# Square roots of the layer norms on ScalarE, and a retention product in three products of parts: one change to a decoder layer on one Trainium2 core

## The chip, the cores and the metric

The kernel runs on one core of a Trainium2 chip. The core has a matrix engine (TensorE, in the profile PE, its weight loads PEld), two engines for elementwise work that matter here (VectorE, DVE, and ScalarE, ACT), a GpSimd engine (POOL) that is all but unused, and a SyncE (SP) that issues most of the DMAs. Each engine works off its own list of instructions in order and waits on semaphores for the others. The metric is the time of one execution in microseconds (us), as the median of several runs.

## The reference, cut to what matters

The layer takes 256 tokens of width 2048. All arrays are float32.

```python
h = layer_norm(alpha * h + 0.5 * swiglu(h, w_ffn1_gu, w_ffn1_down), ln_g[0], ln_b[0])
rq, rk, rv, rg, aq, ak, av, gate_r, gate_a = split(h @ w_in)
ro = head_group_norm(retention_chunkwise(rotary(rq), rotary(rk) * RET_DK**-0.5, rv), ret_gn_g)
ret_branch = (silu(rg) * ro) @ w_ret_out
att_branch = sliding_window_attention_sinks(rotary(aq), rotary(ak), av, att_sinks) @ w_att_out
mixed = (sigmoid(gate_r) * ret_branch + sigmoid(gate_a) * att_branch) @ w_mix_out
h = layer_norm(alpha * h + mixed, ln_g[1], ln_b[1])
h = layer_norm(alpha * h + 0.5 * swiglu(h, w_ffn2_gu, w_ffn2_down), ln_g[2], ln_b[2])
ple = sigmoid(h @ w_ple_gate) * (p @ w_ple_proj)
h = layer_norm(alpha * h + ple, ln_g[3], ln_b[3])
```

`layer_norm` is `(x - mean) * rsqrt(var + 1e-5) * g + b` over the 2048 columns of a token. The retention has 8 heads with keys of 128 and values of 256 columns: a head's output for token t is the sum over s <= t of `gamma**(t-s) * (q_t . k_s) * v_s`, and each head's output is normalized over its 256 columns.

## The kernel before, in words

**Products in parts.** A float32 number is taken as a high part (rounded to the type float32r, which TensorE takes in one pass) and a low part, the remainder, also float32r. `split` (L97) makes both: ScalarE copies the value into the high part, VectorE subtracts it from the value. A product of two such pairs is the sum of three products, low by high, high by high and high by low, in `Sum.add` (L374 to L376). Nearly all of TensorE's work is of this kind, with a weight tile that streams from memory, is split on arrival and is used once. A planner (`plan`, `fill`, `take`, `done`) loads and splits weight chunks ahead of their use, within a budget of buffers; a chunk of weights is 128 by 1024 numbers, its split one ACT and one DVE instruction. After each chunk (a unit of 12 products) `run_side` takes one job from the list `side`; small work that has no stage of its own goes there.

**The layer norms.** There are four, for two halves of 128 tokens (t = 0 and 1) each. Norms 0, 1 and 2 go through the class `Norm`. `held_out` (L506) runs the last product of the stage before for the tokens of t = 0 first, keeping its weight chunks, then `normal(0)` computes the norm of t = 0 on VectorE while TensorE goes through the kept chunks again for t = 1. A written list of events says after which steps `turn` takes place: TensorE transposes 512 normalized columns into a PSUM bank (L593), and `split` makes the next stage's input of them. `normal(1)` follows at the event "sums". The next stage's first chunks are then used in the same order (`first`): t = 0 while the norm of t = 1 is still being made, then t = 1. With norms 0 and 1 a further small product with the embeddings p (`put_by`) stands between the two stages; its results are copied out of PSUM by ScalarE (L737).

`normal(t)` adds the last block of sums (L613), takes its statistics (`bn_stats`, L614), aggregates mean and variance (L576), and calls `rsqrt` (L531) for `1 / sqrt(var + eps)`: eight dependent VectorE instructions on one number per token, which begin with a guess from the bits of the number (L536, L541, L543) and improve it twice (L548, L557, L559, and L548, L561). Then `ln_normal` (L581) applies center-and-multiply (L585) and scale-and-add (L586) to two pieces of 256 columns. The other columns follow in `more`, in pieces of 512.

**The last norm** (`embedding`). The half t = 0 is normalized and stored while TensorE still works on the last product for t = 1. For t = 1, `last_half` (L1465) lets TensorE apply the scale of three blocks of columns: the sums of the block before come from ScalarE's sigmoid (L1428) and VectorE (L1430 to L1432); `ln_stats` gives mean and `rstd`; a row of minus the mean (L1473) and of the deviation (L1474) is transposed by TensorE (L1479), split (L1481, L1484), multiplied with the rows of g and b (L1486) and scaled by `rstd` (L1493, L1495) on the way out.

**The retention.** The values rv (2 blocks of 128 tokens by 2048 columns) are computed in four blocks of 512 columns, and `values` (L1067) copies each out of PSUM in float32. A head's work is a chain of jobs in `side`: `ret1` multiplies keys by queries in float32 (L1111, L1112; 128 by 256 and 128 by 128 scores) and the result by the decay (L1115, L1116); `ret2`, one unit later, multiplies the scores by the values in float32 (L1125 to L1127, three products of 256 columns) and takes statistics; `ret2b`, one more unit later, calls `rsqrt` for both token blocks and normalizes. Two heads follow each other, so six jobs make two heads. These jobs run beside the gate product rg (groups `w_in_f2`), 8 units for two heads, and beside `av` and the first attention features. `ret2c`, `ret3` and `ret3b` gate, transpose and split the result.

**Function tables.** ScalarE loads a table when it changes between functions of different sets. The profiled execution has five such loads: for Silu at the start, for Exp (attention), Sigmoid (gates), Silu (second feed-forward) and Sigmoid (embedding).

Of the kernel before, what the change touches and what calls it, by code (L numbers as in the profile page):

```python
# [8 lines left out]
F32 = mybir.dt.float32  # L9
# [46 lines left out]
def layer(ctx: ExitStack, tc: tile.TileContext, io):  # L56
# [16 lines left out]
    def slot(shape, dt, name):  # L73
        return slots.tile(shape, dt, tag="slot", name=name)
# [456 lines left out]
    def rsqrt(dst, var, n, eps):  # L531
# [7 lines left out]
        )  # L539
        s = small.tile([P, n], I32, tag=f"ns{n}", name="ns")  # L540
        dve.tensor_scalar(s, v[:, 0].bitcast(I32), 1, None, ALU.logical_shift_right)  # L541
        y = small.tile([P, n], I32, tag=f"ny{n}", name="ny")
        dve.tensor_scalar(y, s, -1.0, float(0x5F3759DF - 2**31), ALU.mult, ALU.add)  # L543
# [36 lines left out]

    def ln_normal(y, t, mv, rstd, g, b, k0, nk):  # L581

        x = y[k0 // 4][:, t, k0 % 4 * P : (k0 % 4 + nk) * P]
        at = slice(k0 % 8 * P, (k0 % 8 + nk) * P)
        dve.scalar_tensor_tensor(x, x, mv[:, 0:1], g[k0 // 8][:, at], ALU.subtract, ALU.mult)  # L585
        dve.scalar_tensor_tensor(x, x, rstd, b[k0 // 8][:, at], ALU.mult, ALU.add)  # L586

    def ln_turn(y, t, i, new, k0, nk, keep=None):
# [12 lines left out]
    class Norm:  # L601
# [75 lines left out]
        def first(self, steps, lhs, sums, events):  # L677
# [70 lines left out]
    sink = const.tile([P, HA], F32, name="sink")  # L748
    trig = {}
    ht = big.tile([P, KD, 512], F32R, tag="ht", name="xt")  # L750

# [302 lines left out]
    def mixers(ht, norm, residual, keepers, away):  # L1054
# [52 lines left out]
        def ret1(h):  # L1107
            def f():
# [7 lines left out]
                dve.tensor_tensor(s[:, S:], ps[:, 1, :P], d[:, S:], ALU.mult)  # L1116
                keep["s", h] = s
            return f

        def ret2(h):  # L1120
            def f():
                s = keep.pop(("s", h))
                v = rv[h // 2][:, :, h % 2 * DV : h % 2 * DV + DV]
                ps = bank(f"ro{h}").rearrange("p (a b) -> p a b", a=2)
                pe.matmul(ps[:, 0, :DV], s[:, :P], v[:, 0], start=True, stop=True)  # L1125
# [51 lines left out]
        both = lambda a, b: lambda: (a(), b())  # L1177
        side.append(ret1(0))
        side.append(ret2(0))
        side.append(ret2b(0))  # L1180
        side.append(ret1(1))
        side.append(ret2(1))
        side.append(ret2b(1))
        for h in range(0, HR, 2):
# [12 lines left out]
            if h + 2 < HR:  # L1197
                for n in (h + 2, h + 3):
                    side.append(ret1(n))
                    side.append(ret2(n))  # L1200
                    side.append(ret2b(n))
        aq = [slot([P, 4, S], F32, f"aq{j}") for j in range(2)]
# [218 lines left out]
    def embedding(ht, norm, y):  # L1421
# [43 lines left out]
        def last_half():  # L1465
# [127 lines left out]
    with tc.manual_schedule():  # L1593
        warm = small.tile([P, 1], F32, tag="nc1", name="warm")
        dve.memset(warm, 0.0)
        act.activation(warm, warm, AF.Silu)
        plan_ffn("f1")
# [113 lines left out]
```

## Time and profile before

| what | value |
|---|---|
| median of 3 runs | 2283.61 us (2283.5 to 2283.78) |
| profiled execution, its own time | 2284.39 us |
| span of its instructions | 2282.6 us |
| DVE busy | 1980.0 us, 87% of the span, 2575 instructions |
| ACT busy | 1204.9 us, 53%, 1455 instructions |
| DMA read and written | 478.67 MB and 25.17 MB, 221 GB/s over the span |
| granted TensorE clock | 0.998 |

The profiled execution took 0.78 us more than the median, and its span is 1.79 us shorter than its own time. The profile says of each instruction when it started, how long it took, and what ended the idle time of its engine before it. Matmuls overlap in the pipeline and their ends are modelled, so the distance between two starts is the safer measure on PE.

### The profile page before, as it was taken

The numbers are of one execution on the slowest core, as the hardware profiler recorded it, in microseconds if no ns is written. First come the engines' busy times: TensorE is split into PE (matmuls) and PEld (weight loads), VectorE is DVE, ScalarE is ACT, GpSimd is POOL, SyncE is SP. The second block draws the span as 40 slices with busy tenths as digits, with TensorE's granted clock in tenths as the row PEclk, the third lists the DMA queues.
The fourth block names the chain that finished last, engine by engine and source line by source line (L and its number), as shares of the span: only waits on it lengthen the run. The fifth ranks groups of instructions, "written<-read, shape, count | busy, mean of one in ns | idle before, by whom it ended". The sixth has DMA issues, their size and how long they took to land.

```text
span 2282.6 us, 29021 instructions
## 1 busy us (share of the span) xinstructions
PE 2266.4 (99%) x10471; PEld 1879.7 (82%) x10471; DVE 1980.0 (87%) x2575; ACT 1204.9 (53%) x1455; POOL 2.2 (0%) x9
## 2 busy tenths in 40 slices
PE   9999999999999999999999999999999999999998
PEld 7888888888888888888778888888888888888876
DVE  7999999999989886778789787789999999889877
ACT  5555555556554443535556454555555555555533
POOL 0000000000000000000000000000000000000000
PEclk9999999999999999999999999999999999999999
DMA  8666665665577788655456567777767766565772
GB/s 299 200 207 197 197 211 179 205 202 192 210 284 274 242 304 307 221 161 163 139 157 233 173 221 271 291 272 237 261 221 253 254 199 216 185 220 194 277 259 74
DMA packets 207592, 505.75 MB, mean 222 GB/s; under 512 B 16076, under 2 KB 19788, under 8 KB 207448
## 3 DMA queue, kind: packets, MB, share of 16 engines
q1 hardware_dynamic: 205320, 501.06, 65.3%
q10 hardware_dynamic: 2128, 2.84, 0.4%
q8 instruction: 82, 1.34, 0.2%
q14 instruction: 62, 0.51, 0.1%
HBM read 478.67 MB, written 25.17 MB: 221 GB/s over the span
## 4 chain that ended last, share of the span: by engine, by line
PE 96%; DVE 2%; DMA 1%; issue 0%; ACT 0%; ACTq 0%; DVEq 0%
PE f1g L376 3%; PE f1g L374 3%; PE f1g L375 3%; PE f2g L376 3%; PE f2g L374 3%; PE f2g L375 3%; PE rqk L325 3%; PE f1u L376 2%; PE f1u L374 2%; PE f1u L375 2%; PE f2u L376 2%; PE f2u L374 2%; PE f2u L375 2%; PE aqk L325 2%; PE f2d L374 2%; PE f1d L374 2%
## 5 line engine op out<-in xcount | busy, mean ns | idle before, releaser
L99 DVE TENSOR_TENSOR lf_gu<-rf_gu,hf_gu 128x1024 fp32r<-128x1024 f32 (+1 forms) x276 | 325.3, 1211 | 14.0 <-ACT hf_gu L98 13.2
L98 ACT CAST hf_gu<-rf_gu 128x1024 fp32r<-128x1024 f32 (+1 forms) x276 | 275.5, 1043 | 31.6 <-DMA rf_gu<-in_f_gu 30.7
L99 DVE TENSOR_TENSOR lf_down<-rf_down,hf_down 128x1024 fp32r<-128x1024 f32 x152 | 181.3, 1220 | 23.4 <-ACT hf_down L98 21.1
L99 DVE TENSOR_TENSOR lw_in_f<-rw_in_f,hw_in_f 128x1024 fp32r<-128x1024 f32 x140 | 167.5, 1218 | 35.7 <-ACT hw_in_f L98 35.7
L98 ACT CAST hf_down<-rf_down 128x1024 fp32r<-128x1024 f32 x152 | 155.4, 1050 | 75.7 <-DMA rf_down<-in_f_down 22.2
L98 ACT CAST huf_gu<-uf_gu 128x1024 fp32r<-128x1024 f32 x70 | 73.8, 1054 | 144.9 <-DVE uf_gu L171 142.0
L98 ACT CAST hw_in_f<-rw_in_f 128x1024 fp32r<-128x1024 f32 x140 | 139.2, 1050 | 4.2 <-DMA rw_in_f<-in_w_in_f 1.8
L374 PE MATMUL f1g<-hf_gu,xt 128*128 128x512 f32 x247 | 96.3, 390 | 0.7 <-ACT hf_gu L98 0.7
L376 PE MATMUL f1g<-lf_gu,xt 128*128 128x512 f32 x247 | 96.4, 390 | 0.0
L375 PE MATMUL f1g<-hf_gu,xt 128*128 128x512 f32 x247 | 96.1, 389 | 0.0
L98 ACT CAST hvf_gu<-vf_gu 128x1024 fp32r<-128x1024 f32 x70 | 73.8, 1055 | 29.8 <-DVE vf_gu L173 28.9
L912 ACT ACTIVATE eve<-eve 128x1024 f32<-128x1024 f32 x20 | 21.2, 1061 | 126.8 <-DVE eve L911 126.8
L374 PE MATMUL f2g<-hf_gu,ht 128*128 128x512 f32 x223 | 86.9, 390 | 0.0
L376 PE MATMUL f2g<-lf_gu,ht 128*128 128x512 f32 x223 | 86.8, 389 | 0.0
L375 PE MATMUL f2g<-hf_gu,ht 128*128 128x512 f32 x223 | 86.8, 389 | 0.0
L99 DVE TENSOR_TENSOR luf_gu<-uf_gu,huf_gu 128x1024 fp32r<-128x1024 f32 x70 | 85.3, 1218 | 0.0
L99 DVE TENSOR_TENSOR lvf_gu<-vf_gu,hvf_gu 128x1024 fp32r<-128x1024 f32 x70 | 85.2, 1218 | 0.0
L374 PE MATMUL f1u<-hf_gu,xt 128*128 128x512 f32 x212 | 83.3, 393 | 0.0
L375 PE MATMUL f1u<-hf_gu,xt 128*128 128x512 f32 x212 | 82.5, 389 | 0.0
L376 PE MATMUL f1u<-lf_gu,xt 128*128 128x512 f32 x212 | 82.5, 389 | 0.0
L374 PE MATMUL f2u<-hf_gu,ht 128*128 128x512 f32 x180 | 71.3, 396 | 0.0
L376 PE MATMUL f2u<-lf_gu,ht 128*128 128x512 f32 x180 | 70.1, 390 | 0.0
(1431 smaller groups left out, 6491.2 us busy)
## 6 DMA issues: line engine op xcount, KB each, us to landing
rf_gu<-in_f_gu SPq DMA_DIRECT2D x358, 512.0 KB
rf_down<-in_f_down SPq DMA_DIRECT2D x176, 512.0 KB
rw_in_f<-in_w_in_f SPq DMA_DIRECT2D x148, 512.0 KB
rw_rv<-in_w_rv SPq DMA_DIRECT2D x32, 512.0 KB
rw_ret<-in_w_ret SPq DMA_DIRECT2D x32, 512.0 KB
rw_mix<-in_w_mix SPq DMA_DIRECT2D x32, 512.0 KB
rw_pg<-in_w_pg SPq DMA_DIRECT2D x32, 512.0 KB
rw_att<-in_w_att SPq DMA_DIRECT2D x16, 512.0 KB
```

The costliest lines, as they stand in the source:

```text
L98: act.copy(dst_hi, src)
L99: (lo_engine or dve).tensor_tensor(dst_lo, src, dst_hi, ALU.subtract)
L325: pe.matmul(ps[f], hi[:, kk, f * P : (f + 1) * P], rhs(k), start=k == 0, stop=k == n_k - 1,)
L374: pe.matmul(o, al, bh, start=first, stop=False)
L375: pe.matmul(o, ah, bh, start=False, stop=False)
L376: pe.matmul(o, ah, bl, start=False, stop=self.left == 0)
L912: act.activation(g, g, AF.Silu)
```

## The change

Both halves of norms 0 to 2, and the half t = 1 of the last, get their root from ScalarE: `root = sqrt(4 * var + 4 * eps)`, then VectorE takes the reciprocal and makes one Newton step, four VectorE instructions in all where there were eight. Between the aggregation and the reciprocal VectorE centers the first 256 columns. `Norm.run` loads the table of Sqrt with a one-element activation at its start, and `Norm.first` loads that of the next function at its end. The half t = 0 of the last norm and the heads' norms keep `rsqrt`.

In the retention, `values` splits the values into parts, a new job `ret1b` splits the scores, and `ret2` makes nine products of parts (three for each of the three blocks) in place of three float32 products. The jobs of two heads are interleaved: five entries of `side` instead of six, with two units between a head's `ret1` and its `ret2`.

The tiles `ns` and `ny` get two buffers instead of three, `warm` moves into a constant tile beside the two biases of the roots.

```diff
+    def ln_stats_by_root(stats, i, t, eps, between):
+        mv = small.tile([P, 2], F32, tag="mv", name=f"mv{i}{t}")
+        dve.bn_aggr(mv, stats.rearrange("p a b -> p (a b)"))
+        root = small.tile([P, 1], F32, tag="nq1", name="nroot")
+        act.activation(root, mv[:, 1:2], AF.Sqrt, bias=roots[eps], scale=4.0)
+        v = small.tile([P, 1], F32, tag="nb1", name="nv")
+        dve.tensor_scalar(v, mv[:, 1:2], eps, -4.0, ALU.add, ALU.mult)
+        between(mv)
+        cur = small.tile([P, 1], F32, tag="nc1", name="ncur")
+        dve.reciprocal(cur, root)
+        b = small.tile([P, 1], F32, tag="nh1", name="nb")
+        dve.tensor_scalar(b, cur, cur, v, ALU.mult, ALU.mult)
+        rstd = small.tile([P, 1], F32, tag="rstd", name=f"rstd{i}{t}")
+        dve.scalar_tensor_tensor(rstd, b, 3.0, cur, ALU.add, ALU.mult)
+        return mv, rstd
+
+    def table_of(f):
+        act.activation(warm, warm, f)
...
         def normal(self, t):
             self.columns(t, len(self.cols) - 1)
-            self.mvr[t] = ln_stats(self.stats[:, t], self.i, t, self.eps)
-            for k0 in (0, 2):
-                ln_normal(self.y, t, *self.mvr[t], *self.vectors, k0, 2)
+            g, b = self.vectors
+            self.mvr[t] = ln_stats_by_root(
+                self.stats[:, t], self.i, t, self.eps, lambda mv: ln_center(self.y, t, mv, g, 0, 2)
+            )
+            ln_scale(self.y, t, self.mvr[t][1], b, 0, 2)
+            ln_normal(self.y, t, *self.mvr[t], g, b, 2, 2)
...
             self.vectors = vectors.pop()
+            table_of(AF.Sqrt)
...
             self.put_away()
+            table_of(AF.Silu if self.i < 2 else AF.Sigmoid)
...
         def values(blk, ps):
-            v = slot([P, 2, 512], F32, f"rvs{blk}")
-            act.copy(v[:, 0], ps[0])
-            dve.tensor_copy(v[:, 1], ps[1])
-            rv.append(v)
+            hi, lo = (slot([P, 2, 512], F32R, f"rv{w}{blk}") for w in "hl")
+            for t in range(2):
+                split(hi[:, t], lo[:, t], ps[t])
+            rv.append((hi, lo))
...
+        def ret1b(h):
+            def f():
+                s, parts = keep.pop(("w", h)), slot([P, 2, 384], F32R, f"rsp{h}")
+                split(parts[:, 0], parts[:, 1], s)
+                keep["s", h] = parts
+            return f
...
-                pe.matmul(ps[:, 0, :DV], s[:, :P], v[:, 0], start=True, stop=True)
-                pe.matmul(ps[:, 1, :DV], s[:, P:S], v[:, 0], start=True, stop=False)
-                pe.matmul(ps[:, 1, :DV], s[:, S:], v[:, 1], start=False, stop=True)
+                for t, blks in ((0, ((0, 0),)), (1, ((P, 0), (S, 1)))):
+                    for col, tk in blks:
+                        at = slice(col, col + P)
+                        for a, b in ((1, 0), (0, 0), (0, 1)):
+                            pe.matmul(
+                                ps[:, t, :DV], s[:, a, at], v[b][:, tk],
+                                start=(a, tk) == (1, 0) and col != S, stop=b == 1 and (t, col) in ((0, 0), (1, S)),
+                            )
...
+        def two_heads(h):
+            side.append(ret1(h))
+            side.append(both(ret1b(h), ret1(h + 1)))
+            side.append(both(ret1b(h + 1), ret2(h)))
+            side.append(both(ret2b(h), ret2(h + 1)))
+            side.append(ret2b(h + 1))
...
-            mv, rstd = ln_stats(stats[:, 1], 3, 1, LN_EPS)
+            mv, rstd = ln_stats_by_root(stats[:, 1], 3, 1, LN_EPS, lambda mv: None)
```

More of the change, by code (lines that the diff above doesn't have):

```diff
@@ L539, in rsqrt @@
         )
-        s = small.tile([P, n], I32, tag=f"ns{n}", name="ns")
+        s = small.tile([P, n], I32, tag=f"ns{n}", name="ns", bufs=2)
         dve.tensor_scalar(s, v[:, 0].bitcast(I32), 1, None, ALU.logical_shift_right)
-        y = small.tile([P, n], I32, tag=f"ny{n}", name="ny")
+        y = small.tile([P, n], I32, tag=f"ny{n}", name="ny", bufs=2)
         dve.tensor_scalar(y, s, -1.0, float(0x5F3759DF - 2**31), ALU.mult, ALU.add)
@@ L579, in ln_stats, with ln_center @@
         return mv, rstd
-    def ln_normal(y, t, mv, rstd, g, b, k0, nk):
+    def ln_stats_by_root(stats, i, t, eps, between):
[15 more added lines that the diff above has]
+        act.activation(warm, warm, f)
+    def ln_center(y, t, mv, g, k0, nk):
         x = y[k0 // 4][:, t, k0 % 4 * P : (k0 % 4 + nk) * P]
@@ L585, in ln_normal, with ln_scale @@
         dve.scalar_tensor_tensor(x, x, mv[:, 0:1], g[k0 // 8][:, at], ALU.subtract, ALU.mult)
+    def ln_scale(y, t, rstd, b, k0, nk):
+        x = y[k0 // 4][:, t, k0 % 4 * P : (k0 % 4 + nk) * P]
+        at = slice(k0 % 8 * P, (k0 % 8 + nk) * P)
         dve.scalar_tensor_tensor(x, x, rstd, b[k0 // 8][:, at], ALU.mult, ALU.add)
+    def ln_normal(y, t, mv, rstd, g, b, k0, nk):
+        ln_center(y, t, mv, g, k0, nk)
+        ln_scale(y, t, rstd, b, k0, nk)
     def ln_turn(y, t, i, new, k0, nk, keep=None):
@@ L749, in layer @@
     trig = {}
+    few = const.tile([P, 3], F32, name="few")
+    warm = few[:, 0:1]
+    roots = {LN_EPS: few[:, 1:2], 4 * LN_EPS: few[:, 2:3]}
     ht = big.tile([P, KD, 512], F32R, tag="ht", name="xt")
@@ L1116, in f @@
                 dve.tensor_tensor(s[:, S:], ps[:, 1, :P], d[:, S:], ALU.mult)
-                keep["s", h] = s
+                keep["w", h] = s
+            return f
[4 more added lines that the diff above has]
+                keep["s", h] = parts
             return f
@@ L1122, in f @@
                 s = keep.pop(("s", h))
[L1123 removed]
+                v = [x[:, :, h % 2 * DV : h % 2 * DV + DV] for x in rv[h // 2]]
                 ps = bank(f"ro{h}").rearrange("p (a b) -> p a b", a=2)
[L1125 to L1127 removed]
+                for t, blks in ((0, ((0, 0),)), (1, ((P, 0), (S, 1)))):
[6 more added lines that the diff above has]
+                            )
                 st = small.tile([P, 2, 6], F32, tag="gst", name=f"gst{h}")
@@ L1197, in mixers @@
             if h + 2 < HR:
[L1198 to L1201, printed above, removed]
+                two_heads(h + 2)
         aq = [slot([P, 4, S], F32, f"aq{j}") for j in range(2)]
@@ L1593, in layer @@
     with tc.manual_schedule():
-        warm = small.tile([P, 1], F32, tag="nc1", name="warm")
         dve.memset(warm, 0.0)
+        for eps, v in roots.items():
+            dve.memset(v, 4.0 * eps)
         act.activation(warm, warm, AF.Silu)
```

7 lines of the change are left out of this document (1 added, 6 removed).

## The prediction

> **What bounds the kernel now.** I read three views in this order: the page's busy times, the table of who waited for whom with TensorE as the waiting engine, and the timeline at those places. The columns of the second are: who waits, for whom, us in total, times, longest.
>
> ```profile
> PE 2266.4 (99%) x10471; PEld 1879.7 (82%) x10471; DVE 1980.0 (87%) x2575; ACT 1204.9 (53%) x1455; POOL 2.2 (0%) x9
> ```
>
> ```profile
> PE plnt L1479 <- DVE plnm L1474: 3.7, 1, 3.7
> PE lnps L593 <- DVE mixy L586: 1.9, 4, 0.7
> ...
> PE pg L374 <- DVE ht L99: 1.1, 1, 1.1
> ...
> PE lnps L593 <- DVE f2y L586: 0.6, 2, 0.3
> ```
>
> The reader is to see that TensorE is busy in 99% of the span. Whatever is gained must therefore be either TensorE's own work, or one of its few waits, or a piece of the tail behind its last big product. The waits all stand at layer norms, for a VectorE chain that ends in L586 or L1474. The change touches all three kinds, and nothing else in it can move the end unless it makes TensorE wait anew.
>
> **The retention's products.** One head, and the 256-column products of `av`, on TensorE's timeline (start, duration, line):
>
> ```profile
> 895.74 0.39 PE L376 MATMUL rg<-lw_in_f,ht 128*128 128x512 f32 x1
> 895.97 0.59 PE L1125 MATMUL ro<-rvs,rsc 128*128 128x256 f32 x2
> ...
> 897.49 0.39 PE L375 MATMUL rg<-hw_in_f,ht 128*128 128x512 f32 x1
> ```
>
> ```profile
> 992.29 0.28 PE L374 MATMUL av<-hw_av,ht 128*128 128x256 f32 x1
> ...
> 995.17 0.60 PE L1111 MATMUL rs<-rq,rk 128*128 128x256 f32 x2
> ```
>
> Two steps of the big product take 2 x 0.23 us (895.74 to 895.97 is one), and here 1.75 us pass from L376 to the second product behind the job; so a head's three float32 products cost 1.29 us, 0.43 each. The second fence holds 24 products of parts of 256 columns, each with its own weights, between 992.29 and 995.17: 0.12 us each. Nine of these are 1.08 us. The change **removes 0.21 us per head, 1.7 us for eight**, on TensorE's own path.
>
> What it adds lies on ScalarE and VectorE: per head a split of 128x384 scores, per block of values one more copy and subtraction.
>
> ```profile
> 890.00:1050.00 160.00, 159.97 (x831) 136.35 (x830) 121.36 (x255) 64.57 (x85) 0.00 (x0) 1.00 0.62 199
> ```
>
> ```profile
> 893.76 0.28 DVE L1116 TENSOR_TENSOR rsc<-rs,dec 128x128 f32<-128x128 f32 x1
> ```
>
> ```profile
> 931.07 3.88 ACT L98 CAST hw_in_f<-rw_in_f 128x1024 fp32r<-128x1024 f32 x4
> ```
>
> The first row is the stretch of the heads (length, then busy us of PE, PEld, DVE, ACT): VectorE works 121 of 160 us, ScalarE 65. A split of 1024 columns costs ScalarE 3.88/4 = 0.97 us (the third row), so one of 384 or 512 costs less; eight heads and four blocks add at most 12 us to each engine, which both have free. As for the wait: today the scores are ready at 893.76 + 0.28 = 894.04 and used at 895.97, 1.9 us of slack. The change puts one more unit between (12 products, 2.7 us) and takes a copy and a subtraction (under 1 us each) out of that: about 2.6 us of slack remain. VectorE may have a weight split in front (about 1.2 us), and now and then two. I bound the new waits between 0 and 2 us over eight heads and take 0.3, since the slack is the nearest measured thing. Buffers: the parts hold four slots more for the values and two or three for scores, which delays no weight as long as the planner's lead (over 45 us of queued work by its own count) lasts.
>
> **The chain of a norm.** VectorE at norm 1, t = 0, and the reciprocal of attention:
>
> ```profile
> 1471.11 0.26 DVE L576 BATCH_NORM_AGGREGATE mv<-mixst 128x2 f32<-128x24 f32 x1
> ...
> 1472.68 0.27 DVE L548 TENSOR_SCALAR nb<-ncur,nv 128x1 f32<-128x1 f32 x1
> ...
> 1473.06 0.48 DVE L585 SCALAR_TENSOR_TENSOR mixy<-mixy,mv,ln_g 128x256 f32<-128x256 f32 x1
> 1473.58 0.48 DVE L586 SCALAR_TENSOR_TENSOR mixy<-mixy,rstd,ln_b 128x256 f32<-128x256 f32 x1
> 1473.98 0.48 DVE L585 SCALAR_TENSOR_TENSOR mixy<-mixy,mv,ln_g 128x256 f32<-128x256 f32 x1
> ```
>
> ```profile
> L1266 DVE RECIPROCAL asm<-asm x8: 177/178/179, 1054.0 to 1161.3; 128x4 f32<-128x4 f32 x8
> ```
>
> Today the first scale-and-add starts 1473.58 - 1471.11 = 2.47 us after the aggregation. Afterwards: 0.30 for the aggregation, 0.08 to the centering (an independent instruction follows a tiny one that closely), 0.40 until the next independent one can start (1473.58 to 1473.98), reciprocal 0.20, the two-operand step 0.30, the last step 0.19: 1.47 us. The root on ScalarE starts beside this at 0.30 and takes between 0.21 (a 128x3 activation, quoted below) and 0.33 (half of the 0.66 of the two 256-column sigmoids there); it is done by 0.63, before the reciprocal's turn at 0.78, so it is hidden. **VectorE's chain is 1.0 us shorter in each half.** If ScalarE were held up, that gain would shrink us for us.
>
> How much of it reaches TensorE is read from the distance between the last product before the transposes and the second product after them:
>
> ```profile
> 1477.84 0.39 PE L376 MATMUL pp<-lw_pp,pt 128*128 128x512 f32 x1
> ...
> 1478.74 0.40 PE L375 MATMUL pp<-hw_pp,pt 128*128 128x512 f32 x1
> ```
>
> ```profile
> 716.50 0.39 PE L376 MATMUL rv<-lw_rv,ht 128*128 128x512 f32 x1
> ...
> 718.53 0.39 PE L375 MATMUL rv<-hw_rv,ht 128*128 128x512 f32 x1
> ```
>
> ```profile
> 1473.37 0.39 PE L376 MATMUL mo<-lw_mix,mixt 128*128 128x512 f32 x1
> ...
> 1475.54 0.39 PE L375 MATMUL pp<-hw_pp,pt 128*128 128x512 f32 x1
> ```
>
> ```profile
> 1485.13 0.40 PE L376 MATMUL f2g<-lf_gu,ht 128*128 128x512 f32 x1
> ...
> 1486.53 0.39 PE L375 MATMUL f2u<-hf_gu,ht 128*128 128x512 f32 x1
> ```
>
> ```profile
> 2173.16 0.39 PE L376 MATMUL f2e<-lf_down,f2ah 128*128 128x512 f32 x1
> ...
> 2174.63 0.40 PE L375 MATMUL f2e<-hf_down,f2ah 128*128 128x512 f32 x1
> ```
>
> The first pair is a turn without a wait: 0.90 us. The others take 2.03, 2.17, 1.40 and 1.47, so 1.13 (norm 0, t = 1), 1.27 and 0.50 (norm 1, t = 0 and 1) and 0.57 (norm 2, t = 0) are lost. These losses are longer than the idle times of the wait table because the ends of matmuls are modelled. A chain 1.0 us shorter returns 1.0, 1.0, 0.5 and 0.57; the second wait at f2y (0.24 of the table's 0.6) goes as well, 0.2. The longest wait at mixy (0.7) stays: it stands behind TensorE's own transposes and two ScalarE copies, not behind the root. The wait at `pg` (1.1) hangs on the split of norm 2's second half:
>
> ```profile
> 2187.18 0.65 ACT L98 CAST ht<-lnps 128x256 fp32r<-128x256 f32 x2 [6.49 <-PE lnps L593]
> ```
>
> ```profile
> 2188.01 0.75 DVE L99 TENSOR_TENSOR ht<-lnps,ht 128x256 fp32r<-128x256 f32 x2
> ```
>
> ScalarE's first copy ends near 2187.55 and VectorE comes to it at 2188.01 only because it is late; 1.0 us earlier it meets ScalarE's end, so 0.4 returns and ScalarE is what is late next. **Norms together: 1.0 + 1.0 + 0.5 + 0.57 + 0.2 + 0.4 = 3.7 us.**
>
> **The tables.** A switch shows where the second feed-forward begins, and a gap of ScalarE at norm 1:
>
> ```profile
> 1528.14 1.28 ACT L917 ACT_TABLE_LOAD   x1
> 1529.44 1.09 ACT L917 ACTIVATE f2v<-f2g 128x512 f32<-128x512 f32 x2
> ```
>
> ```profile
> 1474.59 0.37 ACT L596 COPY keep<-lnps 128x256 f32<-128x256 f32 x1 [6.10 <-PE lnps L593]
> ```
>
> A load costs 1.28 us and the next activation follows at once. Sqrt adds four loads, and the returns to other tables are one more than stand there now. At norm 1 ScalarE idles 6.1 us before 1474.59, which covers load and warm activation; without that cover they would cost TensorE up to 1.5 us a norm. The Trainium skill ("ScalarE: Activation LUTs", What ACT_TABLE_LOAD costs) gives 2.66 us for a switch, the load's 1283 ns and a drain of about 1380 ns. By its figure the switch in the tail would be over at 2272.99, the root would start 0.35 late, and the sum below would be 0.35 smaller. The trace agrees with the load's 1283 ns and shows no drain between 1528.14 and 1529.44.
>
> **The tail.** After its last product TensorE waits for the last half:
>
> ```profile
> 2269.67 0.66 ACT L1428 ACTIVATE sg<-pg 128x256 f32<-128x256 f32 x2 [10.29 <-PE pg L376]
> 2272.64 0.21 ACT L1473 ACTIVATE plnm<-mv 128x3 f32<-128x3 f32 x1 [2.31 <-DVE mv L576]
> ```
>
> ```profile
> 2272.34 0.26 DVE L576 BATCH_NORM_AGGREGATE mv<-plst 128x2 f32<-128x24 f32 x1
> ...
> 2274.41 0.17 DVE L1474 SCALAR_TENSOR_TENSOR plnm<-mv,rstd 128x3 f32<-128x3 f32 x1
> ```
>
> L1474 starts 2.07 us after the aggregation. Afterwards, with nothing in between: 0.30, root at most 0.33, reciprocal 0.20, 0.30, 0.20: 1.33. **The tail is 0.7 us shorter**, all of it on the path, since transposition, split, products and stores follow in line. Here no load is asked for ahead: it is placed before the root. The sigmoids end at 2270.33, so a load of 1.28 is over at 2271.61, 1.0 us before the variance. If it only began once the root's wait was over, the tail would lose 0.6 instead.
>
> **The sum.** 1.7 - 0.3 + 3.7 + 0.7 = 5.8 us off the profiled execution's 2284.39 (span 2282.6 and 1.79 around it): 2278.6. That execution was 0.78 over the median, so the median comes to 2277.8.
>
> **Rivals.**
> - *The norms' gain stays on VectorE.* If TensorE meets another late thing behind the same transposes (as at `pg`, where ScalarE is next), only 1.4 + 0.7 and a little of the 3.7 remain: 2281.0. For it: the mixy wait of 0.7 has nothing to do with the root. Against: the quoted waits end at L586 directly.
> - *Nine products are bound by their weight loads.* At 0.19 us each a head would take 1.71 and the gain of 1.7 become a loss of 3.4; with norms and tail 2282.6. Against it stand the 24 products of `av`.
> - *Slower: the split of the scores comes late.* If ScalarE's copy stands behind a run of four weight casts (3.88 us at 931.07) and VectorE's subtraction behind two splits (2.4), the 2.6 us of slack are overdrawn by some 1.5 to 2 us in a head; over eight heads 12 to 16 us, 2290 to 2294. It decides from 0.75 us of waiting per head on, where eight heads eat the other terms' 6.1 us. Against it: casts run ahead of TensorE, and ScalarE would stop at the scores' copy before, not behind, the later casts.
> - *A switch takes longer than its load.* If it took two loads' time, 2.56 us, the one in the tail would end at 2272.89, the root would start 0.25 late: 2278.1. Against it stands the activation at 1529.44. The Trainium skill's section named above has such a rule.
>
> **How the numbers follow.** Forecast 0.70, norms hidden 0.13, longer switch 0.07, weight loads 0.05, slower 0.05. A measurement of this kernel can tell about 0.2% from no change, 4.6 us, which is 2279.0. The longer switch and 0.61 of the forecast's 0.70 are below that (its three terms all have to hold); 0.09 of the forecast, hidden norms and weight loads are within. So faster 0.68, same 0.27, slower 0.05. The range's low end takes every quoted loss back in full and no waits in the retention (1.7 + 4.2 + 0.8, and 0.9 for waits that the view doesn't name): 2276.0. Its high end is the hidden case with its spread, 2281.4.
>
> **What would show it.** `ro` starts 0.12 us apart and no TensorE wait on `rsp`; transposes of norms 0 and 1 without waits but for one of 0.7; the scale-and-add 1.5 us behind the aggregation; the last table load before 2272; L1474 1.3 us behind its aggregation. A wait on `rsp` above 0.75 us a head, or a root that starts late, would make the prediction wrong.

## The result, and the profile after

The changed kernel takes 2277.11 us (median of 9 runs, 2276.6 to 2277.95), the kernel before, run beside it, 2283.5 us (9 runs, 2282.19 to 2284.55). The ratio is 0.9973, with a 95% interval of 0.9962 to 0.9983; the medians are 6.4 us apart. The forecast was 2277.8. The profiled execution of the changed kernel took 2277.11 us with a span of 2275.3. Of all the executions told of here one, of the kernel before beside the second group of experiments, took 13135.89 us; it is left out of that group's median.

The busy times of the page, and the table of who waited for whom with TensorE as the waiting engine (us in total, times, longest):

```profile
PE 2263.4 (99%) x10495; PEld 1880.2 (83%) x10495; DVE 1980.6 (87%) x2561; ACT 1219.5 (54%) x1485; POOL 2.2 (0%) x9
```

```profile
PE plnt L1529 <- DVE plnm L1524: 2.9, 1, 2.9
...
PE lnps L623 <- DVE mixy L611: 0.7, 1, 0.7
PE pg L374 <- DVE ht L99: 0.7, 1, 0.7
...
PE lnps L623 <- DVE f2y L611: 0.5, 2, 0.3
PE rt L1212 <- DVE ron L1203: 0.2, 1, 0.2
```

Three things are to be seen. The waits at `f1y` are gone and of four at `mixy` one is left, the one of 0.7. The wait in the tail fell from 3.7 to 2.9 and that at `pg` from 1.1 to 0.7. No wait on `rsp` was added, but a small one of `rt` was. TensorE's busy time fell by 3.0 us (2266.4 to 2263.4) although it has 24 instructions more (a float32 product counted as two).

One head of the retention on TensorE and VectorE, and the split of its scores on ScalarE:

```profile
890.86 0.59 PE L1149 MATMUL rs<-rq,rk 128*128 128x256 f32 x2
...
897.66 0.40 PE L1174 MATMUL ro<-rvh,rsp 128*128 128x256 f32 x2
897.89 0.28 PE L1174 MATMUL ro<-rvl,rsp 128*128 128x256 f32 x1
898.01 0.40 PE L1174 MATMUL ro<-rvh,rsp 128*128 128x256 f32 x2
898.25 0.28 PE L1174 MATMUL ro<-rvl,rsp 128*128 128x256 f32 x1
```

```profile
892.42 0.51 ACT L98 CAST rsp<-rsc 128x384 fp32r<-128x384 f32 x1 [1.60 <-DVE rsc L1154]
```

```profile
893.38 0.55 DVE L99 TENSOR_TENSOR rsp<-rsc,rsp 128x384 fp32r<-128x384 f32 x1
```

Three products lie between 897.66 and 898.01: 0.12 us each. The parts are ready at 893.38 + 0.55 = 893.93 and used at 897.66, 3.73 us later.

The chain of norm 1, t = 0, on VectorE, with ScalarE beside it:

```profile
1467.66 0.26 DVE L585 BATCH_NORM_AGGREGATE mv<-mixst 128x2 f32<-128x24 f32 x1
1467.95 0.15 DVE L589 TENSOR_SCALAR nv<-mv 128x1 f32<-128x1 f32 x1
1468.03 0.47 DVE L606 SCALAR_TENSOR_TENSOR mixy<-mixy,mv,ln_g 128x256 f32<-128x256 f32 x1
1468.42 0.15 DVE L592 RECIPROCAL ncur<-nroot 128x1 f32<-128x1 f32 x1
...
1469.11 0.48 DVE L611 SCALAR_TENSOR_TENSOR mixy<-mixy,rstd,ln_b 128x256 f32<-128x256 f32 x1
```

```profile
1465.06 1.28 ACT L601 ACT_TABLE_LOAD   x1
1466.35 0.20 ACT L601 ACTIVATE few<-few 128x1 f32<-128x1 f32 x1
1467.95 0.29 ACT L587 ACTIVATE nroot<-mv,few 128x1 f32<-128x1 f32 x1 [1.40 <-DVE mv L585]
```

From aggregation to the first scale-and-add it is 1469.11 - 1467.66 = 1.45 us, where 1.47 was forecast. The root ends at 1467.95 + 0.29 = 1468.24, before VectorE comes to the reciprocal at 1468.42.

The tail:

```profile
2264.05 0.66 ACT L1478 ACTIVATE sg<-pg 128x256 f32<-128x256 f32 x2 [10.29 <-PE pg L376]
2264.72 1.28 ACT L587 ACT_TABLE_LOAD   x1
2267.01 0.30 ACT L587 ACTIVATE nroot<-mv,few 128x1 f32<-128x1 f32 x1 [1.00 <-DVE mv L585]
```

```profile
2266.71 0.26 DVE L585 BATCH_NORM_AGGREGATE mv<-plst 128x2 f32<-128x24 f32 x1
...
2268.03 0.17 DVE L1524 SCALAR_TENSOR_TENSOR plnm<-mv,rstd 128x3 f32<-128x3 f32 x1
```

The load begins right behind the sigmoids, while the root still has to wait for the variance, and it is over at 2266.00. L1524 starts 1.32 us behind the aggregation; 1.33 was forecast.

**Where the 7.29 us between the two spans went.** For this I compared the starts of the same TensorE instructions in both traces, stage by stage:

| stage | forecast | measured | from the start of (before, after) |
|---|---|---|---|
| start of the kernel | - | 0.67 | first turn of norm 0: 703.05, 702.38 |
| norm 0 | 1.0 | 1.05 | last turn: 726.54, 724.82 |
| retention | 1.4 | 1.56 | `ga0a` behind it: 1173.07, 1169.79 |
| norm 1 | 1.5 | 1.71 | last turn: 1498.70, 1493.71 |
| norm 2 | 1.2 | 0.63 | first `pln` behind it: 2269.47, 2263.85 |
| tail, to `plnt` | 0.7 | 0.77 | 2274.73, 2268.34 |
| last products | - | 0.23 | last L1486 (L1536): 2276.71, 2270.09 |
| to the end of the span | - | 0.67 | 2282.61, 2275.32 |

The forecast terms add up to 5.8, and their stages gave 5.72. The other 1.57 us fell where the change has nothing: a wait near the start, the last three products, and the time after them, in which the results are stored. The 0.23 of the three products goes back to the moment at which TensorE's granted clock fell (last section). The row of the first is in the table of waits of the kernel before:

```profile
PE f1g L374 <- ACT hf_gu L98: 0.7, 1, 0.7
```

### The profile page after: what moved, and what is told of

The parts are those of the page before. It is cut to its first block, busy times and chain, and to the rows that moved or that the text cites. A ratio compares the mean times of both kernels' runs of the same rounds, so it can differ in the third digit from the quotient of the medians.

```text
span 2275.3 us, 29066 instructions
## 1 busy us (share of the span) xinstructions
PE 2263.4 (99%) x10495; PEld 1880.2 (83%) x10495; DVE 1980.6 (87%) x2561; ACT 1219.5 (54%) x1485; POOL 2.2 (0%) x9
## 3 DMA queue, kind: packets, MB, share of 16 engines
q8 instruction: 82, 1.34, 0.2%
## 4 chain that ended last, share of the span: by engine, by line
PE 97%; DVE 1%; DMA 1%; issue 0%; ACT 0%; POOL 0%; ACTq 0%; DVEq 0%; POOLq 0%
PE f1g L375 3%; PE f1g L374 3%; PE f1g L376 3%; PE f2g L376 3%; PE f2g L374 3%; PE f2g L375 3%; PE rqk L325 3%; PE f1u L374 2%; PE f1u L376 2%; PE f1u L375 2%; PE f2u L374 2%; PE f2u L376 2%; PE f2u L375 2%; PE aqk L325 2%; PE f1d L374 2%; PE f1d L376 2%
```

## The experiments

Intervals of these ratios are some 0.1% (2 us) to each side, so a single microsecond is not read from the times alone. I read it from the traces, place by place, and use the medians as a check. Every experiment's time stands beside that of the kernel before on the same chip: 2283.54 for the first four (27 runs), 2283.8 for the next four (24 runs), 2283.66 for the last three (15 runs). The length of a turn is, as in the prediction, the distance from the last product ahead of its transposes to the second product behind them; without a wait it is 0.90 us.

**The kernel before, once more** (no edit).

> The kernel before once more, for a second profile of it. Between the two profiled executions 7.29 us of span went, 1.3 more than the terms account for. Theory A (two pieces of it have nothing to do with the change): the 0.7 us in which TensorE waits for the first cast of hf_gu near the start, and the 4.49 us from the start of the last instruction on VectorE that works on the output to the end of the span (3.81 after), differ from execution to execution; so in this second profile at least one of the two differs by 0.3 us or more from the first, while the turns of the norms keep their distances of 2.03, 2.18, 1.40 and 1.47 us within 0.05 and L1474 starts 2.07 us after the aggregation within 0.03. Rival B (both belong to the kernel before, and the change takes them away by a way not seen yet): the wait is 0.7 and the end 4.5 again, within 0.1 each. One more thing to read: the three last products of TensorE (L1486) begin 0.59 and 0.43 apart here and 0.36 and 0.43 in the changed kernel. If the longer idle time ahead of them in the kernel before (3.7 us against 2.9 at plnt) makes the difference, 0.59 comes again.

One execution, 2282.91 us, span 2281.1. Its table of waits of TensorE begins:

```profile
PE plnt L1479 <- DVE plnm L1474: 3.7, 1, 3.7
PE lnps L593 <- DVE mixy L586: 1.5, 3, 0.7
PE warm L1591 <- POOL ident masks.py:199: 1.4, 1, 1.4
PE pg L374 <- DVE ht L99: 1.1, 1, 1.1
```

The wait at `f1g` doesn't occur at all, and from the end of VectorE's last instruction to the end of the span it is 4.10 us, where the first profile had 4.49 (the expectation says that 4.49 is counted from that instruction's start; it is from its end). Over the thirteen profiles of this study that last stretch is 3.69 to 4.49 us, whatever the kernel. So theory A holds: those two pieces come and go with the execution. Against this second profile the changed kernel's span is 5.8 us shorter. What I hadn't expected is that the losses at the norms vary too. Of the four turns that the expectation names two miss its bound of 0.05, norm 1's first with 1.79 us (2.18 in the first profile) and norm 2's first with 1.36 (1.47); and norm 0's first, which had no loss there, takes 1.24 (0.90). The 0.59 between the last products came again.

**Roots alone.**

```diff
 the changed kernel, with values, ret1, ret2 and the order of side jobs as before
```

> The roots of ScalarE with their table loads, in the norms and in the tail, without the products of parts. Theory A (the terms are separate and add up): the three norms give 1.05 + 1.71 + 0.64, the tail 0.75 and 0.2 at its last products, so 4.3 us less than the kernel before, near 2279.2; TensorE's turns stand at 1.00, 1.02, 0.90 and 1.32 us as in the changed kernel. Rival B (the retention's copies and subtractions, by loading ScalarE and VectorE, or the wait for the split scores, took part of the norms' gain away): over 5 us less than before, under 2278.5. Rival C (most of the gain is in the products): under 3 us less, over 2280.5.

2278.14 us (11 runs), ratio 0.9978 (0.9969 to 0.9987), 5.4 us less than before. This is over theory A's 4.3 and meets rival B's figure, but the trace speaks against B: the turns take 1.01 (norm 0), 0.91 and 0.90 (norm 1) and 1.18 us (norm 2), the tail waits 2.9. Against the second profile of before, the spans differ by 4.46 us, and the distances at the norms and the tail account for 4.1 of them. The first turns of norms 1 and 2 are 0.11 and 0.14 better than in the changed kernel's profile. Norm 2's moves by more than that between executions of one kernel (below). At norm 1 two kernels further down that do have the products, the one without tables asked for ahead and the one with only the table behind, take 0.91 as well, so the products are not what costs that 0.11, and nothing in these runs is left for B.

**Products alone.**

```diff
 the kernel before, with values, ret1, ret1b, ret2 and two_heads of the changed one
```

> The retention's products of parts with their two units' distance, old norms and old tail. Theory A: eight heads of three float32 products at 0.43 us become nine products at 0.12, 0.21 less each and no wait, 1.5 to 1.7 us less than the kernel before, near 2281.9; the stretch between the product ahead of the first head and that behind the last is 1.5 shorter, and the norms lose what they lost before (2.03, 2.18, 1.40, 1.47). Rival B (products bound by weight loads, or waits for the split): no gain, 2283.5 or more. Rival C (the parts free time for the norms as well): over 2.5 us less, under 2281.

2282.5 us (11 runs, 2281.01 to 2283.53), ratio 0.9994 (0.9985 to 1.0003): 1.0 us less, less than theory A had, and not clear of no change. In the trace the retention, between the marks of the table above, is 1.5 us shorter, as theory A had it. The norms don't keep all their losses, though: norm 1's first turn takes 1.82 us, and norm 2's first takes 3.12, 1.65 more than in the profile of before. ScalarE and VectorE just ahead of it:

```profile
2160.83 1.05 ACT L98 CAST hw_pg<-rw_pg 128x1024 fp32r<-128x1024 f32 x1 [1.81 <-DMA rw_pg<-in_w_pg]
2164.33 1.05 ACT L98 CAST hw_pg<-rw_pg 128x1024 fp32r<-128x1024 f32 x1 [2.45 <-DMA rw_pg<-in_w_pg]
```

```profile
2165.41 1.22 DVE L99 TENSOR_TENSOR lw_pg<-rw_pg,hw_pg 128x1024 fp32r<-128x1024 f32 x1 [1.75 <-ACT hw_pg L98]
2166.55 0.68 DVE L990 TENSOR_TENSOR f2y<-f2y,f2e 128x512 f32<-128x512 f32 x1
```

A weight for a later product landed late, its split stood on VectorE ahead of the norm's statistics, and those waited 1.75 us for it. The retention's gain stands in its stage; here it was lost again 1,100 us later, to the time of a transfer. In the other ten profiles that have this turn in its place it takes 0.91 to 1.65 us, and this once 3.12. Whether every execution of this kernel has it is not shown.

**The old distance.** The split in the job of the scores, the nine products one unit later.

```diff
-            side.append(ret1(h))
-            side.append(both(ret1b(h), ret1(h + 1)))
-            side.append(both(ret1b(h + 1), ret2(h)))
-            side.append(both(ret2b(h), ret2(h + 1)))
-            side.append(ret2b(h + 1))
+            for n in (h, h + 1):
+                side.append(both(ret1(n), ret1b(n)))
+                side.append(ret2(n))
+                side.append(ret2b(n))
```

> The changed kernel with the old distance in the retention: each head's scores are split in the job that makes them, and its nine products stand in the next unit of TensorE's work instead of the one after. In the changed kernel the parts of a head's scores are ready 2.2 us after its last score product starts and are used 2.9 us (with the unit more between) after that. Theory A (there is slack for it: the split ends about 0.3 us or more ahead of the next job): TensorE waits for rsp in few heads or none, under 1 us over all eight, and the time stays within 1 us of the changed kernel's 2277.1; the second unit was not needed. Rival B (the split comes late behind weight casts on ScalarE and splits on VectorE): 0.75 us and more of waiting in a head, 6 us and more over eight, 2283 and above.

2280.18 us (11 runs), 3.1 more than the changed kernel. Neither figure was met.

```profile
PE ro L1174 <- DVE rsp L99: 1.9, 2, 1.4
...
PE rt L1212 <- DVE ron L1203: 1.0, 1, 1.0
```

Six of eight heads have their parts 0.68 to 0.91 us before use and don't wait. The third waits 1.36 and the fourth 0.57, and the transposes of gated heads behind them another 1.0. The stretch of the retention shows why the third is late:

```profile
928.38 0.48 DVE L1224 SCALAR_TENSOR_TENSOR rett<-rt,gn,rett 128x256 fp32r<-128x256 f32 x1 [0.54 <-ACT rett L1223]
929.32 1.22 DVE L99 TENSOR_TENSOR lw_in_f<-rw_in_f,hw_in_f 128x1024 fp32r<-128x1024 f32 x1 [0.45 <-ACT hw_in_f L98]
930.46 0.42 DVE L1153 TENSOR_TENSOR rsc<-rs,dec 128x256 f32<-128x256 f32 x1
```

The scores are on VectorE's list behind the parts of an earlier head and a weight's split, each of which waited for ScalarE first. In the changed kernel the same head is the tightest one: its parts are ready 1.78 us ahead of use, while the eight heads have 1.78 to 4.15 (the expectation's 2.9 is the figure of none of them). So the unit more is needed, for two heads of eight.

The retention is 2.9 us longer by the marks of the table. In this profile another 0.7 us went at norm 1, whose first turn takes 1.73 us where the changed kernel's takes 1.02, and the start of the kernel was 0.65 shorter. VectorE ahead of that turn shows why it is late:

```profile
1468.01 1.23 DVE L99 TENSOR_TENSOR lf_gu<-rf_gu,hf_gu 128x1024 fp32r<-128x1024 f32 x1 [1.33 <-ACT hf_gu L98]
```

This split of a weight for the next stage stands ahead of the norm's last columns and statistics, and ScalarE's cast for it had waited 1.50 us for the weight's transfer. So norm 1's first turn, too, can hang on when a weight lands.

**No tables asked for ahead.**

```diff
-            table_of(AF.Sqrt)
...
-            table_of(AF.Silu if self.i < 2 else AF.Sigmoid)
```

> The changed kernel without the two calls that ask for a table ahead of and behind each norm: the tables then change where the next function needs it, at the first root of a norm and at the next Silu or Sigmoid behind it. Theory A (a table's load is not held back by the wait of the activation that follows it, as in the tail, where the load starts 0.02 us behind the sigmoid and 2.29 ahead of the root): ScalarE idles 2.7 us and more ahead of each norm's first root, the load stands in that gap, and the time stays within 0.5 us of the changed kernel's 2277.1. Rival B (the load starts with the root's wait over): the first root of each norm comes 1.28 us later, 0.9 to 1.2 of it reach TensorE at norms 0, 1 and 2 each, 2280 or more.

2278.4 us (10 runs), 5.4 less than before where the changed kernel has 6.4. At the norms theory A holds: turns of 1.01, 0.91 and 0.90 us, and the three loads start 0.02 us behind the last cast, not with the root. The total is 1.0 off all the same, twice theory A's bound. The loss is in the retention, which is 1.5 us longer than in the changed kernel's trace:

```profile
PE rt L1210 <- DVE ron L1201: 1.4, 2, 0.8
```

```profile
912.51 1.99 ACT L98 CAST hw_in_f<-rw_in_f 128x1024 fp32r<-128x1024 f32 x2
914.52 1.28 ACT L1241 ACT_TABLE_LOAD   x1
915.82 1.09 ACT L1241 ACTIVATE rgs<-rg 128x512 f32<-128x512 f32 x2
```

The changed kernel's ScalarE has the first gates at 914.48. Here they come 1.34 us later, behind the load of their table, the product with the gates on VectorE comes 1.35 us later, and TensorE waits 1.4 in two transposes.

**Only the table behind the norm asked for.**

```diff
-            table_of(AF.Sqrt)
```

> The changed kernel without the call ahead of each norm that asks for the root's table, but with the one behind it that asks for the table of Silu or Sigmoid. Theory A (the load for the root stands in idle time of ScalarE wherever it is asked for, and the 1.3 us that both calls together are worth come from the call behind norm 0 alone: without it the load of Silu's table stands between two casts and the first gates of the retention, at 914.5, and the transposes of gated heads wait): no wait of rt for ron over 0.3, time within 0.4 us of the changed kernel on the same chip. Rival B (the call ahead of the norms is worth something): 0.9 us or more above it.

2277.57 us (9 runs), against 2277.31 for the changed kernel on the same chip, and the `rt` wait is the changed kernel's again:

```profile
PE rt L1211 <- DVE ron L1202: 0.2, 1, 0.2
```

So the call ahead of the norms is worth nothing that these runs can tell, and the calls behind them the 1.0 us of the times, or the 1.5 of the traces. By the place of the wait it is the one behind norm 0; the other two were not taken out alone.

**A switch that can't hide**, in the tail alone.

```diff
         dve.bn_aggr(mv, stats.rearrange("p a b -> p (a b)"))
+        if i == 3:
+            act.activation(warm, mv[:, 1:2], AF.Sigmoid)
         root = small.tile([P, 1], F32, tag="nq1", name="nroot")
```

> The changed kernel with one more activation in the tail alone: a sigmoid of the variance ahead of the root, so that the switch to the root's table can begin only once the variance is there. Nothing uses its result. Theory A (a switch is its load of 1.28 us and nothing more): sigmoid 0.3, load 1.28, then the root; the root starts 1.6 us later than today and the tail is 1.6 longer: 2278.7. Rival B (a drain of the pipeline of about 1.4 us stands between, as the Trainium skill's page ScalarE: Activation LUTs has it in the section What ACT_TABLE_LOAD costs): 3.0 longer, 2280.1.

2278.99 us (11 runs), 4.8 less than before: 1.6 us of the changed kernel's gain are gone.

```profile
2266.99 0.20 ACT L587 ACTIVATE few<-mv 128x1 f32<-128x1 f32 x1 [2.31 <-DVE mv L585]
2267.20 1.28 ACT L589 ACT_TABLE_LOAD   x1
2268.50 0.29 ACT L589 ACTIVATE nroot<-mv,few 128x1 f32<-128x1 f32 x1
```

The root starts 1.51 us behind the sigmoid: 0.20 for it, 1.28 for the load, 0.03 between them. The wait at `plnt` grows from 2.9 to 4.4 us. Theory A holds. The drain of about 1.38 us in the Trainium skill ("ScalarE: Activation LUTs", What ACT_TABLE_LOAD costs) isn't there, neither as idle time of ScalarE nor in the end; its 1283 ns for the load is what the trace has.

**The old tail.**

```diff
-            mv, rstd = ln_stats_by_root(stats[:, 1], 3, 1, LN_EPS, lambda mv: None)
+            mv, rstd = ln_stats(stats[:, 1], 3, 1, LN_EPS)
```

> The changed kernel with VectorE's three steps for the root in the last half alone (norms and retention as changed). Theory A (the tail is all on the path): L1524's counterpart starts 2.07 us behind the aggregation instead of 1.32, the time is 0.75 longer, 2277.9. Rival B (a store or TensorE's own products set the end): under 0.2 longer, 2277.3 or less.

2278.22 us (10 runs), 5.6 less than before, so 0.8 of the gain belongs to the tail, as theory A had it. Its table of waits says the same:

```profile
PE plnt L1529 <- DVE plnm L1524: 3.7, 1, 3.7
```

**The changed kernel once more** (no edit).

> The changed kernel once more, on the chip of the two kernels below, as the mark that they are measured by, and for a second profile of it. Theory A (the terms belong to the change): turns of 1.00, 1.02, 0.90 and 1.32 us, 1.32 from aggregation to L1524, ro 0.12 apart, each within 0.05 but for norm 2's first turn, whose place depends on when the last weights land (1.18 to 1.65 in the runs so far); 2276.9 to 2277.6, and the last three products begin 0.59 and 0.43 apart as in all kernels but that one profile. Rival B (the 5.8 of the terms was luck of one profile): terms off by over 0.3 in sum.

2277.31 us (7 runs), ratio 0.9972 (0.9961 to 0.9983). Turns of 1.00, 1.04, 0.90; norm 2's first takes 0.91 (1.32 in the first profile), its second 1.31; 1.32 us in the tail; 0.59 and 0.43 between the last products. So the 0.36 of the first profile was of that execution. At the norms, in the two kernels' four profiles, it is first turns that depend on the execution: norm 2's in the changed kernel (0.91 and 1.32), those of all three norms in the kernel before. Summed over the five stages that the forecast names, each of the two profiles of the changed kernel is 5.6 to 6.1 us shorter than each of the two of before.

**Later turns**, twice: what is left at the turns of norms 1 and 2, put elsewhere. The second edit, which contains the first but for one number:

```diff
             ln_normal(self.y, t, *self.mvr[t], g, b, 2, 2)
+            if (self.i, t) == (2, 0):
+                self.more(0, 1)
...
-            if c < 3 and (t, c + 1) != self.put_off:
+            late = self.i == 2 and (t, c) == (1, 0)
+            ahead = (self.i, t, c) == (2, 0, 0)
+            if c < 3 and (t, c + 1) != self.put_off and not late and not ahead:
...
                     ln_turn(*args, k0, 2, self.keep.get(c))
+                if late:
+                    self.more(t, c + 1)
...
-                    (3, (1, 0)), (5, (1, 1)), (6, "more"), (7, (0, 2)), (8, (1, 2)), (9, (0, 3)), (10, (1, 3)), (10, "go"),
+                    (3, (1, 0)), (5, "more"), (5, (1, 1)), (7, (0, 2)), (8, (1, 2)), (9, (0, 3)), (10, (1, 3)), (10, "go"),
...
-            norm.run(steps, lhs, ((8, (0, 0)), (11, (0, 1))))
+            norm.run(steps, lhs, ((9, (0, 0)), (11, (0, 1))))
...
-                    (1, (0, 2)), (1, "sums"), (6, (1, 0)), (7, (1, 1)), (8, (1, 2)), (8, "more"), (9, (1, 3)),
+                    (1, (0, 2)), (1, "sums"), (5, (1, 0)), (7, (1, 1)), (8, (1, 2)), (8, "more"), (9, (1, 3)),
```

The first version has neither `ahead` nor the early `more(0, 1)`, and (12, (0, 1)) where this one has (11, (0, 1)).

> The changed kernel with the turns that still wait put elsewhere, all arithmetic the same: at norm 1 the pieces (0, 2) are normalised ahead of turn (1, 1) and not behind it; at norm 2 turn (0, 0) stands one step later, (0, 1) one step later, and (1, 0) one step earlier with the next piece's normalising behind its own split. Theory A (these waits only stand where TensorE asks too early, and VectorE has time before): of the losses left, 0.96 at norm 1's (0, 2), 0.42 and 0.49 at norm 2's first two turns go, and of 0.97 at pg about 0.5; together 1.9 to 2.4 us, near 2275.0. Rival B (VectorE or ScalarE is itself the bound there, so the wait only moves to the next turn): under 0.6 us less, 2276.5 or more.

2275.87 us (5 runs), ratio 0.9964 (0.9951 to 0.9977): 7.9 less than before, so 1.5 beyond the changed kernel, a bit under theory A. Norm 1's (0, 2) went from 1.86 to 0.90 us and the wait at `pg` is no longer in the table. Norm 2's second turn stayed at 1.40 although it stands a step later, and the third grew from 0.90 to 1.19: at this one place rival B's picture. VectorE in the changed kernel shows what the turn waits for:

```profile
2168.84 0.68 DVE L1028 TENSOR_TENSOR f2y<-f2y,f2e 128x512 f32<-128x512 f32 x1
2169.55 0.70 DVE L644 BATCH_NORM_STATS2 f2st<-f2y 128x6 f32<-128x512 f32 x1
2170.16 0.74 DVE L606 SCALAR_TENSOR_TENSOR f2y<-f2y,mv,ln_g 128x512 f32<-128x512 f32 x1
2170.93 0.75 DVE L611 SCALAR_TENSOR_TENSOR f2y<-f2y,rstd,ln_b 128x512 f32<-128x512 f32 x1
```

The sums and statistics of the other half, which nobody needs soon, stand ahead of the piece that TensorE is about to transpose. The second version turns that order round.

> The kernel with later turns, but at norm 2 the second piece of the first half is normalised right behind the first, ahead of the other half's columns, and its turn stands where the changed kernel has it (after step 11). Theory A (the wait of 0.49 there came from the order on VectorE, columns ahead of the piece, not from VectorE being full): that turn 0.90 to 0.95, the next one 0.90, so 0.8 us below the kernel with later turns and 2.0 to 2.5 below the changed kernel on the same chip. Rival B (VectorE is the bound): the wait goes to another turn, under 1.6 us below the changed kernel.

2275.09 us (5 runs, 2274.64 to 2275.39), ratio 0.9963 (0.9950 to 0.9975), 2.2 us under the changed kernel on the same chip. Norm 2's first two turns take 0.91 and 0.90 us, the third 1.00, and of the waits of TensorE only these are left above 0.5:

```profile
PE plnt L1535 <- DVE plnm L1530: 2.9, 1, 2.9
PE warm L1647 <- POOL ident masks.py:199: 1.4, 1, 1.4
PE pln L1542 <- DVE plnst L1540: 0.7, 1, 0.7
```

It was VectorE's order, not its load. This version beats both kernels, with the same arithmetic as the changed one.

## Why the prediction was right, step by step

The forecast time was 0.7 us off, and the mechanism is the one that was forecast: three separate terms that add up. Roots alone give 5.4 us and products alone 1.0, together 6.4, as much as the whole change. With 2 us to each side, and the 1.65 that the second lost at norm 2, that agreement is in part luck; the traces carry the point better, with 4.1 at the norms and the tail for the one and 1.5 in the retention for the other.

The first reading, that all waits stand at layer norms, was too broad: the rows left out of the prediction's table hold two that don't, 1.4 at `warm` and the 0.7 at `f1g`. The change touches neither, so no term hangs on it.

- **Retention, 1.4 forecast, 1.56 measured (1.5 with products alone).** Nine products at 0.12 us in place of three at 0.43 came out as worked out from the rows of `av`; the rival of 0.19 per product is refuted by the starts of `ro`. The 0.3 for new waits was 0.2, but at another place: not `rsp`, but the transposes of gated heads, `rt`, and only where the new products are. The slack of 2.6 us lies in a wide spread, 1.78 to 4.15, of which six heads of eight have 3.7 or more: it was read off one head, and the tight ones are others. The slower rival's waiting is real, but it needs a unit less, it hits two heads of eight, and the thing in front is VectorE's list ahead of the scores' product, not four casts ahead of the copy.
- **Norms, 3.7 forecast, 3.4 measured.** VectorE's chain became 1.0 us shorter (2.47 to 1.45). Norms 0 and 1 gave a little more than forecast, 2.76 for 2.5, but how it divides between them is of the execution: against the second profile of before it would be 1.45 and 1.33 in place of 1.05 and 1.71, since norm 1's loss of 1.27 was 0.89 there. `pg` gave the 0.4. Two items of norm 2 failed. The 0.57 of its first turn was 0.15 in this profile and would be 0.56 by the changed kernel's second one. Two experiments above (norm 2's first turn with products alone, norm 1's with the old distance) show that such a turn can hang on when a weight lands; for the difference between these two profiles that is not shown. The 0.2 of the second `f2y` wait was 0: I had put it down to the root, and it stood behind the other half's columns, as the last experiment shows. The rival that the norms' gain stays on VectorE is refuted but for these two.
- **Tables, nothing forecast.** True for the loads ahead of the roots, with or without the call that asks for them. I priced the return to Silu at nothing as well without looking for its place, and only a call behind the norm makes that so: without it 1.0 us go by the times, 1.5 by the traces. The longer switch is refuted.
- **Tail, 0.7 forecast, 0.77 measured** in the trace, 0.8 by the time of the old tail.
- **The sum.** 5.8 forecast, 5.72 in the stages that it named; 6.4 between the medians. Of the 7.29 between the two profiled spans 1.57 belong to the two executions. The range's low end counts the quoted losses as 4.2 where they add up to 4.1; nothing hangs on it. What the 0.7 between 5.7 and 6.4 is, is not settled. That the kernel before loses more than its profile showed in some executions, at norms whose first turns vary by 0.3 to 0.4 us, would fit, and so would chance: the interval of the ratio is 2.4 us to each side.

## What to carry to other kernels

Where TensorE is busy in 99% of the span, a shorter chain on another engine is worth what TensorE loses at that chain's end and no more; the distance between the last product before and the second one after shows it better than the idle time does. Before pricing a wait, read what stands ahead of the late instruction on its own engine: at three places here (norm 1's later turn, norm 2's second turn, `pg`) a wait went when a few pieces changed their place in that list, which was worth 2.2 us, more than the products. When a function brings a new table, look at both switches; the one back is the one that may stand in front of work that is waited for.

## What the runs showed of the hardware

- A table's load isn't held back by the wait of the activation behind it: in all kernels every load but the first starts within 0.02 us of the end of ScalarE's instruction ahead of it, in the tail 2.29 us before its root can start. A switch that can't hide costs its 1.28 us and 0.03 more.
- The three last products, 66 x 512 columns, begin 0.57 to 0.59 and 0.43 us apart in ten of thirteen profiles, but 0.36 and 0.43 in the first of the changed kernel, 0.35 and 0.38 with the old tail, 0.34 and 0.23 in the last kernel. The granted clock of TensorE, the share of its full clock that it gets, goes with all thirteen. It falls from 1.0 to 0.5 once in each trace, during the wait at `plnt` or up to 1.9 us behind its end, 2.8 to 5.0 us after the end of TensorE's product ahead of that wait. From the second of the three to the third, first in the changed kernel's first profile, then in the last kernel's (stretch, length, TensorE's busy time and instructions, granted clock, the transfers' share and rate):

```profile
2269.66:2270.09 0.43, 0.43 (x2) 0.50 0.00 0
```

```profile
2267.30:2267.53 0.23, 0.23 (x3) 1.00 0.00 0
```

In the ten profiles the clock has fallen before the first of the three begins, or falls within 0.05 us behind that; in the first profile of the changed kernel it falls between the first and the second, with the old tail just behind the start of the second, in the last kernel only behind the start of the third. So from the start of the first to that of the third it is 1.02 us where the clock falls early, and 0.57 where it falls late. The second profile of the changed kernel has 0.59 behind the same 2.9 us at `plnt`: there it fell 1.0 us ahead of the first of the three. Why it falls earlier or later is not shown.
